# A transformer layer with an expert lookup on one Trainium2 core: SBUF sums for three output blocks only, a fourth gate tile loaded a block ahead, and a fourth tile for loads of u and v

## The chip, the cores and the metric

The kernel runs on one core of a Trainium2 chip. The metric is the device time of one execution in microseconds (us); before the change it is 3120.34 us, the median of three runs (3112.70 to 3122.46 us). A core has five engines with an instruction stream each: PE multiplies matrices, DVE (VectorE) and ACT (ScalarE) work on whole tiles, POOL (GpSimd) here issues gathers of table rows, and SP (SyncE) here issues nearly all other DMA transfers. Each stream is executed in its order, so an instruction that waits holds up everything behind it on that engine. SBUF holds 128 partitions of on-chip memory, PSUM the sums of PE.

## The reference, cut to what matters

One layer is computed for 1024 tokens of width 1024: attention, a convolution branch and, at the end, a product-key expert lookup, which takes most of the time. For each token 8 heads select 16 of 16384 experts each, with weights g, and

```
ue = take(u_tab, idx); ve = take(v_tab, idx)          # 128 rows of 1024 for each token
act = gelu(einsum('thkd,td->thk', ue, t))
out = einsum('thk,thkd->td', g * act, ve)
```

## The kernel before, in words

The tokens are two halves of 512. For the expert part the kernel does not gather rows for most tokens. It goes through all 16384 experts in 128 chunks of 128 and computes for all tokens of a half at once: `ups` = u chunk times h2 (24 matmuls, since each factor is split into two fp16 parts), `gel` = gelu of it, times a dense gate matrix that is zero where an expert was not selected, split into `wdh` (ACT) and `wdl` (DVE). The result times the v chunk is added to eight output blocks d of 128 rows. SUB = 4 chunks make a group, and a group's outputs are computed while the next group's chunks are prepared (`dense`).

Half 0 (`hf` = 0) does this for 512 tokens. Half 1 does it for 384 tokens and without `ups`: for these the products of u rows were gathered by POOL and multiplied on DVE beside half 0 (`dots`, tile `row`), and they are already in the gates. The last 128 tokens are done by gathers of u and v rows alone (`rows_out`, tile `racc`).

The gates lie in DRAM (`gd`, written by `build_g` from tile `ge`). They are read in blocks of GR = 8 chunks by two loads, one for each half q of the tokens, into tiles `gt`, of which there are three. `chunk` issues both loads when it comes to the first chunk of a block (lines 1081 to 1090). Loads of u and v (512 KB each) share the tag `uv32` with three tiles (lines 1096, 1105). Of the eight output blocks of half 0, five are kept in PSUM over all groups (`res`, NRES = 5); for the other three PE fills a `vps` bank in each group, which DVE adds to the SBUF tile `acc0`. `acc0` has room for all eight blocks (16 KB in each partition, line 1376). After half 0, `final` turns `acc0` into the output, while half 1 runs.

The order of the work around the change is made by a scheduler (Tile) that takes the instructions as the program lists them, with their tiles and pools, and sets the order in each engine's stream by its own estimate. A new tile of a tag, or a new pool at the address of a closed one, waits until what was there before is used up. `run_side` weaves the side streams (gates, gathered rows) between the steps of `dense`. Before the expert part come the key scores of half 1 (`scores`: tiles `sl`, `qql`, results `sv`, `si`), whose pools are closed just before the dense pools open; three chunks of u are split ahead (`u_first`, tiles `whl`).

Of the kernel before, what the change touches and what calls it, by code (L numbers as in the profile page):

```python
# [8 lines left out]
F32 = mybir.dt.float32  # L9
F16 = mybir.dt.float16  # L10
# [3 lines left out]
AF = mybir.ActivationFunctionType  # L14
# [4 lines left out]
D = 1024  # L19
L = 1024  # L20
CTX = 256
HALF = 512
# [5 lines left out]
TB = 8  # L28
REP = 4
NDENSE = 512  # L30
NMIX = 384
LATE_DOTS = 34
GATES_B = 0.64
GATES_D = 0.072
AHEAD = 1
GR = 8
DVE_ROWS = ((), tuple(range(8)), (), (1, 2, 3, 4, 5, 7))
W_FIRST = 6
UPRE = 3
SUB = 4  # L40
NGR = 128 // SUB
NRES = 5
# [67 lines left out]
class K:  # L110
# [841 lines left out]
    def build_g(self, t, hf):  # L952

        nc, p = self.nc, self.pg
        yield
        yield
        ii, g16 = self.slots(t, hf)
        yield
        late = []
        for q in range(128 // 16):  # L960
            ge = p.tile([128, 128, 16], F32, name="ge", tag="ge", bufs=self.ge_bufs)
            for sub in range(16 // TB):
                t0 = q * 16 + sub * TB
                ts = slice(t0, t0 + TB)

                def onehot(name, src, idx, op):
                    x = p.tile([128, TB, 128 // REP, REP], F16, name=name, tag=name, bufs=2)
                    nc.vector.tensor_tensor(x, src, idx[:, ts].unsqueeze(2).to_broadcast([128, TB, 128 // REP, REP]),
                                            op=op)
                    return x  # L970

                e1 = onehot("e1", self.iota, ii[:, 0], ALU.is_equal)
                ah = onehot("ah", e1, g16[:, 0], ALU.mult)
                al = onehot("al", e1, g16[:, 1], ALU.mult)
                e2 = onehot("e2", self.iota, ii[:, 1], ALU.is_equal)
# [27 lines left out]
    def open_gate(self, name, side, ge_bufs):  # L1003
        nc, a = self.nc, self.a
        self.ge_bufs = ge_bufs
        g, self.pg = self.pool(name, side=side)
        p = self.pg
        io32 = p.tile([128, 128], F32, name="io32")
        nc.sync.dma_start(io32, a["iota"])
        io16 = p.tile([128, 128], F16, name="iotas")  # L1010
        nc.vector.tensor_copy(io16, io32)
        self.iota = io16.rearrange("p (a b) -> p a b", b=REP).unsqueeze(1).to_broadcast([128, TB, 128 // REP, REP])
        self.cand = p.tile([128, 8, NCAND], F32, name="cand", tag="cand", bufs=1)
        nc.vector.memset(self.cand[:, :, 16:128], NEG)
        self.iota16 = p.tile([128, 16, 16], F16, name="iota16")
        nc.vector.tensor_copy(self.iota16, io32[:, 0:16].unsqueeze(2).to_broadcast([128, 16, 16]))
        return g
# [54 lines left out]
                pass  # L1072


    def chunk(self, hf, i1, p, pv):
# [5 lines left out]
        if self.gblock != (hf, i1 // GR):  # L1081
            self.gblock = hf, i1 // GR
            self.gts = []
            for q in range(2):
                gt = p.tile([128, nb, GR, 16], F32, name="gt", tag="gt", bufs=3)
                nc.sync.dma_start(
                    gt.rearrange("p b i t -> p b (i t)"),
                    self.gd[hf][nb * q:nb * q + nb].rearrange("b p i t -> p b (i t)")
                    [:, :, i1 // GR * GR * 16:(i1 // GR + 1) * GR * 16])
                self.gts.append(gt)  # L1090
        early = hf == 0 and i1 < UPRE
        if hf == 0 and not early:
            if i1 in self.u_first:
                uh, ul = self.u_first[i1]
            else:
                u32 = p.tile([128, 8, 128], F32, name="u32", tag="uv32", bufs=3)
                nc.sync.dma_start(u32, a["u_t"][i1])
                uh = p.tile([128, 8, 128], F16, name="uh", tag="uh", bufs=2)
                ul = p.tile([128, 8, 128], F16, name="ul", tag="ul", bufs=2)
                self.split(u32, 256.0, uh, ul)  # L1100
        late = []
        if hf and i1 in self.vparts:
            vh, vl = self.vparts[i1]
        else:
            v32 = p.tile([128, D], F32, name="v32", tag="uv32", bufs=3)
            nc.sync.dma_start(v32, a["v"][i1 * 128:(i1 + 1) * 128, :])
            vh = p.tile([128, D], F16, name="vh", tag="vh", bufs=2 * SUB)
            vl = p.tile([128, D], F16, name="vl", tag="vl", bufs=2 * SUB)
            nc.scalar.activation(vh, v32, AF.Copy, scale=16.0)  # L1109
            late.append((vl, v32, 16.0, vh))  # L1110
            if i1 >= 128 - 2 * SUB:
                self.vparts[i1] = vh, vl
        wh = self.pac.tile([128, nt], F16, name="wdh", tag="wdh", bufs=2 * SUB)
        wl = p.tile([128, nt], F16, name="wdl", tag="wdl", bufs=2 * SUB)
        if hf == 0:
            ge = p.tile([128, nt], F32, name="gel", tag="gel", bufs=2)
            if early:
                nc.sync.dma_start(ge, self.ged[i1])
            else:
                ps = pv.tile([128, 512], F32, name="ups", tag="v", bufs=3)  # L1120
                for k in range(8):
                    self.mm3(ps, uh[:, k, :], ul[:, k, :], hh[:, k, :], hl[:, k, :], k == 0, k == 7)
                nc.scalar.activation(ge, ps, AF.Gelu, scale=2.0 ** -12)
            gev = ge.rearrange("p (b t) -> p b t", t=16)
            for q in range(2):
                qs = slice(nb * q, nb * q + nb)
                nc.vector.tensor_mul(gev[:, qs, :], gev[:, qs, :], self.gts[q][:, :, i1 % GR, :])
            nc.scalar.activation(wh, ge, AF.Copy, scale=256.0)  # L1128
            late.append((wl, ge, 256.0, wh))
        else:  # L1130
            for q in range(2):
                qs = slice(nb * q, nb * q + nb)
                g = self.gts[q][:, :, i1 % GR, :]
                wq = wh.rearrange("p (b t) -> p b t", t=16)[:, qs, :]
                nc.scalar.activation(wq, g, AF.Copy, scale=256.0)
                late.append((wl.rearrange("p (b t) -> p b t", t=16)[:, qs, :], g, 256.0, wq))
        self.anchor = nc.vector.last
        for x in late:
            self.lo(*x)
        return vh, vl, wh, wl  # L1140

    def outputs(self, hf, gi, d, chunks, acc, pv):

        nc = self.nc
        nt = (NDENSE, NMIX)[hf]
        dsl = slice(d * 128, (d + 1) * 128)
        first, last = gi == 0, gi == NGR - 1
        if hf:
# [8 lines left out]
        po = po[:, :nt]  # L1157
# [3 lines left out]
        ad = acc[:, d, :nt]  # L1161
        if keep:
            if last:
                nc.scalar.activation(ad, po, AF.Copy)
        elif first:
            nc.vector.tensor_copy(ad, po)
        else:
            nc.vector.tensor_add(ad, ad, po)

    def outputs_mix(self, first, last, d, chunks, pv):  # L1170

# [16 lines left out]

    def dense(self, p, pv, accs):

        self.res, self.mix, self.vparts, self.gblock = {}, {}, {}, None
        prev = None
        for hf in range(2):
            for gi in range(NGR):
# [101 lines left out]
    def experts(self, p, pv, acc0):  # L1296

        rows = self.rows_stream()
        accs = [acc0, None]
# [3 lines left out]
        accs[1] = self.pc.tile([128, 8, HALF], F32, name="acc1", tag="h2")  # L1303
        self.run_side(self.ends(main, acc0, p), rows=rows, rate=(128 + LATE_DOTS) / 374.0)
        for _ in rows:
            pass
        self.last_group(accs[1], p, pv)

    def ends(self, main, acc0, p):
        last = self.final(acc0, p)  # L1310
# [7 lines left out]
    def run(self):  # L1318
# [60 lines left out]
        self.experts(pd, pv, acc0)  # L1379
        self.close(gd)  # L1380
        self.close(g_ac)
        self.close(g_g)
# [65 lines left out]
```

## Time and profile before

| what | value |
|---|---|
| three runs | 3112.70, 3120.34, 3122.46 us |
| profiled execution, own time | 3120.57 us |
| its span, first to last instruction | 3118.8 us |
| busy PE, DVE, ACT, POOL | 2913.7, 2631.9, 1180.7, 1067.5 us |
| mean granted PE clock | 0.977 |
| DMA moved | 795.75 MB, mean 255 GB/s |

Times in the profile count from the first instruction. The expert part starts with the first `ups` matmul at 1110.6 us; half 0 ends with the last `ups` at 2517.7 us. Busy time of PE is modelled: matmuls overlap at their ends. The granted clock is a share of the full 2.4 GHz; the lower level is 1.2 GHz, so a mean between 0.5 and 1 is a mix of both. "DMA" in a table of stretches is the mean busy share of the 16 DMA engines.

### The profile page before, as it was taken

To read this page: it belongs to the slowest core of one execution; us is meant where nothing else is said; L and a number is where in the kernel's file an instruction comes from. 1 tells how busy PE (TensorE), PEld (TensorE's weight loads), DVE (VectorE), ACT (ScalarE), POOL (GpSimd) and SP (SyncE) were. 2 spreads that over 40 slices of the span, in tenths; PEclk is the share of its full clock that TensorE was granted. 3 is DMA by queue.
4 is the path that set the end of the run, shared out by engine and by line. 5 is a ranking of instruction groups with operands and counts; after the bars stand their busy time and mean duration, and the time that the engine had idled before them with its cause. 6 is when DMAs were issued, how large, how long until landed. Compare 5 with 4: busy or idle time off the path is not lost. (4 is left out here: it accounts for less than half of the span.)

```text
span 3118.8 us, 49200 instructions
## 1 busy us (share of the span) xinstructions
PE 2913.7 (93%) x18685; PEld 1534.6 (49%) x18685; DVE 2631.9 (84%) x5438; ACT 1180.7 (38%) x1878; POOL 1067.5 (34%) x812
## 2 busy tenths in 40 slices
PE   6899999998899989999999999999999999999998
PEld 2455555444454444443444444344444456666665
DVE  7788666698899999899799988889988988777687
ACT  4744566333444332322333332333332333433332
POOL 2100011202231004444444544444444443444453
PEclk9999999999999999999999999999999999999999
DMA  6333334653445628898899998889898989999996
GB/s 218 95 110 111 112 116 152 234 183 136 174 191 196 234 87 307 280 317 303 303 316 335 345 325 297 295 318 342 315 335 304 336 287 341 328 323 326 333 321 225
DMA packets 327198, 795.75 MB, mean 255 GB/s; under 512 B 22961, under 2 KB 147249, under 8 KB 319793
## 3 DMA queue, kind: packets, MB, share of 16 engines
q1 hardware_dynamic: 222992, 397.25, 38.1%
q0 software_dynamic: 103968, 395.36, 34.8%
q8 instruction: 146, 2.39, 0.3%
q14 instruction: 92, 0.75, 0.1%
HBM read 696.31 MB, written 96.21 MB: 254 GB/s over the span
## 5 line engine op out<-in xcount | busy, mean ns | idle before, releaser
L904 POOL DMA_INDIRECT row<-u,ci x512 | 680.5, 1329 | 920.9 <-DVE row L67 685.0
L67 DVE SCALAR_TENSOR_TENSOR row<-row,hn 128x1024 f32<-128x1024 f32 x512 | 620.6, 1226 | 80.9 <-DMA row<-u,ci 75.0
L67 PE MATMUL res<-wdl,vh 128*128 128x128 f16 (+2 forms) x2176 | 629.3, 306 | 28.1 <-DVE wdl L67 28.0
L67 PEld LDWEIGHTS <-vh 128*128 128x128 f16 x5120 | 469.2, 98 | 340.0 <-issue 11.3
L67 PE MATMUL res<-wdh,vh 128*128 128x128 f16 (+2 forms) x2176 | 625.1, 306 | 3.3 <-ACT vh L1109 1.7
L67 PE MATMUL res<-wdh,vl 128*128 128x128 f16 (+2 forms) x2176 | 625.7, 306 | 0.8 <-DVE vl L67 0.8
L67 PE MATMUL ups<-h,uh 128*128 128x512 f16 x1952 | 589.8, 384 | 21.9 <-DVE acc L67 12.8
L67 PEld LDWEIGHTS <-whl 128*128 128x128 f16 x3288 | 315.1, 99 | 367.9 <-issue 41.9
L1109 ACT ACTIVATE vh<-v 128x1024 f16<-128x1024 f32 x248 | 258.4, 1052 | 484.9 <-DMA v<-v 433.6
L67 PE MATMUL ups<-h,ul 128*128 128x512 f16 x976 | 374.9, 384 | 21.1 <-DVE ul L67 21.1
L67 PE MATMUL bank<-hT,whl 128*128 128x512 f16 x1584 | 375.5, 386 | 15.7 <-ACT hT L331 5.7
L67 PEld LDWEIGHTS <-vl 128*128 128x128 f16 x2560 | 251.5, 98 | 205.0 <-issue 37.2
L67 DVE SCALAR_TENSOR_TENSOR vl<-v,vh 128x1024 f16<-128x1024 f32 x248 | 300.1, 1222 | 55.6 <-ACT vh L1109 53.1
L67 PEld LDWEIGHTS <-uh 128*128 128x128 f16 x1952 | 192.8, 99 | 258.0 <-issue 36.6
L904 POOL DMA_INDIRECT row<-v,ci x128 | 200.5, 1566 | 220.8 <-DVE racc L67 197.7
L140 ACT ACTIVATE uh<-u 128x1024 f16<-128x1024 f32 x122 | 128.4, 1052 | 311.1 <-PE ups L67 255.3
L1128 ACT ACTIVATE wdh<-gel 128x512 f16<-128x512 f32 x128 | 80.3, 629 | 371.4 <-DVE gel L67 353.3
L67 DVE SCALAR_TENSOR_TENSOR racc<-row,fig,racc 128x1024 f32<-128x1024 f32 x127 | 163.0, 1283 | 10.7 <-DMA row<-v,ci 9.7
L67 PEld LDWEIGHTS <-ul 128*128 128x128 f16 x976 | 96.6, 99 | 141.6 <-DVE ul L67 23.5
L67 DVE SCALAR_TENSOR_TENSOR ul<-u,uh 128x1024 f16<-128x1024 f32 x122 | 148.6, 1221 | 15.2 <-ACT uh L140 15.1
L67 PEld LDWEIGHTS <-e 128*128 128x128 f16 x1792 | 114.4, 99 | 94.4 <-issue 37.5
L67 DVE TENSOR_TENSOR e<-iotas,ii 128x1024 f16<-128x1024 f16 x224 | 145.4, 691 | 18.2 <-PE fbank L67 13.1
(230 smaller groups left out, 4192.6 us busy)
## 6 DMA issues: line engine op xcount, KB each, us to landing
v<-v SPq DMA_DIRECT2D x248, 512.0 KB, 6.5
u<-u_t SPq DMA_DIRECT2D x122, 512.0 KB, 6.7
gd<-ge POOLq DMA_DIRECT2D x32, 1024.0 KB, 4.4
gt<-gd SPq DMA_DIRECT2D x32, 1024.0 KB, 13.6
wm<-w_mod SPq DMA_DIRECT2D x48, 512.0 KB, 4.3
gd<-ge SPq DMA_DIRECT2D x24, 1024.0 KB, 8.6
gt<-gd SPq DMA_DIRECT2D x32, 768.0 KB, 11.0
w<-w_in SPq DMA_DIRECT2D x34, 512.0 KB, 4.2
```

The costliest lines, as they stand in the source:

```text
L67: r = f(*args, **kw)
L140: nc.scalar.activation(h, src, AF.Copy, scale=float(scale))
L904: self.nc.gpsimd.indirect_dma_start(out=r, out_offset=None, in_=tab, in_offset=bass.IndirectOffsetOnAxis(ap=ci[:, s:s + 1], axis=0))
L1109: nc.scalar.activation(vh, v32, AF.Copy, scale=16.0)
L1128: nc.scalar.activation(wh, ge, AF.Copy, scale=256.0)
```

## The change

Gate loads are issued by `load_gates`, for the next block, when chunk 2 (q = 0) and chunk 5 (q = 1) of the present block are listed, and there are four `gt` tiles. The tag `uv32` has four tiles. The room comes from `acc0`: during half 0 only three blocks have SBUF sums, in the tile `part`; the whole `acc0` is made at the end of half 0 at the address of h2, which is no longer read then, and `acc1` at the same address after it. `e1` of the gate builder has one tile in place of two, and the iota load shares the tile of `dot`.

```diff
+GATE_AT = (2, 5)
-                    x = p.tile([128, TB, 128 // REP, REP], F16, name=name, tag=name, bufs=2)
+                    x = p.tile([128, TB, 128 // REP, REP], F16, name=name, tag=name, bufs=1 if name == "e1" else 2)
-        io32 = p.tile([128, 128], F32, name="io32")
+        io32 = p.tile([128, 128], F32, name="io32", tag="dot", bufs=1)
+    def load_gates(self, hf, blk, q, p):
+        nb = (NDENSE, NMIX)[hf] // 32
+        if (hf, blk, q) not in self.gtiles:
+            gt = p.tile([128, nb, GR, 16], F32, name="gt", tag="gt", bufs=4)
+            self.nc.sync.dma_start(
...
+            self.gtiles[hf, blk, q] = gt
     def chunk(self, hf, i1, p, pv):
...
-            for q in range(2):
-                gt = p.tile([128, nb, GR, 16], F32, name="gt", tag="gt", bufs=3)
-                nc.sync.dma_start(
...
+            for q in range(2):
+                self.load_gates(hf, blk, q, p)
+            self.gts = [self.gtiles.pop((hf, blk, q)) for q in range(2)]
+        nxt = blk - 1 if hf else blk + 1
+        if 0 <= nxt < 128 // GR:
+            for q in range(2):
+                if (i1 + hf * SUB) % GR == GATE_AT[q]:
+                    self.load_gates(hf, nxt, q, p)
-                u32 = p.tile([128, 8, 128], F32, name="u32", tag="uv32", bufs=3)
+                u32 = p.tile([128, 8, 128], F32, name="u32", tag="uv32", bufs=4)
-            v32 = p.tile([128, D], F32, name="v32", tag="uv32", bufs=3)
+            v32 = p.tile([128, D], F32, name="v32", tag="uv32", bufs=4)
...
-        elif first:
+            return
+        ad = self.part[:, d - NRES, :]
+        if first:
             nc.vector.tensor_copy(ad, po)
         else:
-            nc.vector.tensor_add(ad, ad, po)
+            nc.vector.tensor_add(acc[:, d, :] if last else ad, ad, po)
...
+    def whole_acc(self, name):
+        return self.pc.tile([128, 8, HALF], F32, name=name, tag="h2")
...
-        acc0 = self.pac.tile([128, 8, HALF], F32, name="acc0")
+        self.part = self.pac.tile([128, 8 - NRES, HALF], F32, name="part")
```

In SP's stream of before, in half 1 at the start of a block: `gt_29143` is the second half of the block whose first chunk has the v tile `v32_29145`; `gt_29562` is the first half of the block after it.

```order
L1106 DMA v32_29078<-v 128x1024
L1106 DMA v32_29145<-v 128x1024
L1106 DMA v32_29187<-v 128x1024
L1106 DMA v32_29226<-v 128x1024
L1086 DMA gt_29143<-gd384_93 128x12x128
L1086 DMA gt_29562<-gd384_93 128x12x128
```

The same place in the changed kernel: `gt_29226` and `gt_29396` are both halves of the block after, whose first chunk has `v32_29566`.

```order
L1119 DMA v32_29145<-v 128x1024
L1119 DMA v32_29187<-v 128x1024
L1119 DMA v32_29228<-v 128x1024
L1119 DMA v32_29291<-v 128x1024
L1081 DMA gt_29226<-gd384_93 128x12x128
L1081 DMA gt_29396<-gd384_93 128x12x128
L1119 DMA v32_29354<-v 128x1024
L1119 DMA v32_29398<-v 128x1024
L1119 DMA v32_29437<-v 128x1024
L1119 DMA v32_29500<-v 128x1024
L1119 DMA v32_29566<-v 128x1024
```

A half of a block that stood three rows behind the v load of its own first chunk now stands five rows ahead of it; both halves stand together at the border of the block before, not at its chunks 2 and 5.

SP's stream of before, where the expert part begins: the loads of the first chunks (`gt_11995`, `v32_11999`, `gel_12006`) stand between the last weights of the score stage (`whl`).

```order
L1086 DMA gt_11995<-gd512_92 128x16x128
L1086 DMA gt_11997<-gd512_92 128x16x128
L800 DMA h2d_89<-hn_11306 128x4x128
L157 DMA whl_11418<-ws_sk1_6811 128x2048
L1106 DMA v32_11999<-v 128x1024
L1118 DMA gel_12006<-ged0_10238 128x512
L157 DMA whl_11455<-ws_wq9_6853 128x2048
L1106 DMA v32_12024<-v 128x1024
```

The same place in the changed kernel, from the last weight on:

```order
L158 DMA whl_11851<-ws_wq15_7279 128x2048
L161 DMA w32_11963<-u_t 128x1024
L1010 DMA io32_11987<-iota 128x128
L914 DMA hn2_12442<-h2d_89 128x1024
L1081 DMA gt_11995<-gd512_92 128x16x128
L1081 DMA gt_11997<-gd512_92 128x16x128
L1119 DMA v32_11999<-v 128x1024
L1131 DMA gel_12006<-ged0_10238 128x512
L1119 DMA v32_12024<-v 128x1024
L1131 DMA gel_12031<-ged1_10272 128x512
L1081 DMA gt_12048<-gd512_92 128x16x128
L1119 DMA v32_12050<-v 128x1024
```

All loads of the expert part moved behind all loads of the score stage. The first of them, `gt_11995`, now lies where `whl` and `w32` tiles were, and it waits for the last `ups` matmul that reads the third split chunk of u (`whl_11962`).

DVE's stream of before in the score stage has work of the first chunks between two rounds of the key search (`sl`):

```order
L67 MAX_INDEX si1_86<-sv1_85,sl_11433 128x8 x4
L67 TENSOR_TENSOR gel_12006<-gel_12006,gt_11995 128x256
L67 TENSOR_TENSOR gel_12006<-gel_12006,gt_11997 128x256
L67 SCALAR_TENSOR_TENSOR vl_12002<-v32_11999,vh_12001 128x1024
L67 SCALAR_TENSOR_TENSOR qql_11483<-bank_11457,qqh_11482 128x512
L67 MAX sv1_85<-sl_11499 128x8 x4
```

In the changed kernel it stands behind the last round (`sl_11930`):

```order
L68 MAX_INDEX si1_86<-sv1_85,sl_11930 128x8 x4
L68 MEMSET cand_11991 128x8x112
L68 TENSOR_SCALAR g2r_30863<-g2s_83 128x8
L68 CAST iotas_11989<-io32_11987 128x128
L68 CAST iota16_11993<-io32_11987 128x256
L68 TENSOR_TENSOR gel_12006<-gel_12006,gt_11995 128x256
L68 TENSOR_TENSOR gel_12006<-gel_12006,gt_11997 128x256
L68 SCALAR_TENSOR_TENSOR vl_12002<-v32_11999,vh_12001 128x1024
```

Seven `vl`, one `ul` and four `gel` instructions left the score stage in this way.

## Rows read from the trace of the kernel before

**Rows 1.** The page's first line: span of the profiled execution.
```profile
span 3118.8 us, 49200 instructions
```
**Rows 2.** Busy time by stretch: length, engines' busy (instructions), PE clock, DMA share, GB/s.
```profile
1130.00:1200.00 70.00, 62.29 (x279) 27.46 (x278) 59.84 (x187) 21.31 (x28) 18.45 (x15) 0.95 0.55 184
1200.00:2518.00 1318.00, 1266.81 (x6283) 590.86 (x6282) 1172.70 (x2053) 420.19 (x566) 608.42 (x459) 0.98 0.89 316
...
2560.00:3096.00 536.00, 506.95 (x4538) 351.20 (x4536) 416.81 (x585) 192.59 (x371) 248.29 (x163) 0.98 0.91 321
```
**Rows 3.** Waits of PE, 2560 to 3096: sum in us, times, longest.
```profile
PE res L67 <- DVE wdl L67: 26.5, 16, 3.4
```
**Rows 4.** Waits of ACT in the same stretch.
```profile
ACT wdh L1135 <- DMA gt<-gd: 109.7, 14, 10.9
```
**Rows 5.** Waits of DVE in the same stretch.
```profile
DVE wdl L67 <- ACT wdh L1135: 67.6, 13, 9.3
```
**Rows 6.** Timeline of SP's DMA issues at one block's start: start, length, what.
```profile
2740.34 3.46 SPq L1086 DMA_DIRECT2D gt<-gd  x2
```
**Rows 7.** Timeline of ACT, same place; in brackets the idle time before.
```profile
2750.73 0.36 ACT L1135 ACTIVATE wdh<-gt 128x192 f16<-128x192 f32 x1 [9.90 <-DMA gt<-gd]
```
**Rows 8.** Timeline of PE, same place.
```profile
2761.34 0.48 PE L67 MATMUL res<-wdl,vh 128*128 128x384 f16 x1 [3.42 <-DVE wdl L67]
```
**Rows 9.** Busy time by stretch, right behind that wait.
```profile
2760.00:2768.00 8.00, 6.66 (x24) 3.30 (x24) 6.91 (x8) 3.63 (x8) 5.80 (x5) 0.57 0.93 336
```
**Rows 10.** Waits of DVE in half 0, 1200 to 2518.
```profile
DVE row L67 <- DMA row<-u,ci: 58.8, 60, 3.8
DVE vl L67 <- ACT vh L1109: 24.7, 10, 6.1
DVE wdl L67 <- ACT wdh L1128: 24.3, 9, 4.7
DVE ul L67 <- ACT uh L140: 15.1, 13, 2.2
DVE gel L67 <- DMA gt<-gd: 9.1, 4, 3.0
```
**Rows 11.** Timeline of ACT in half 0, where a load of v is late.
```profile
1271.79 1.06 ACT L1109 ACTIVATE vh<-v 128x1024 f16<-128x1024 f32 x1 [11.65 <-DMA v<-v]
1272.75 0.61 ACT L1128 ACTIVATE wdh<-gel 128x512 f16<-128x512 f32 x1
```
**Rows 12.** Busy time by stretch from the score stage to the first outputs.
```profile
1060.00:1100.00 40.00, 35.93 (x218) 18.16 (x217) 40.00 (x207) 13.88 (x20) 0.00 (x0) 1.00 0.51 176
1100.00:1110.00 10.00, 3.88 (x32) 2.54 (x31) 10.00 (x43) 3.86 (x7) 0.00 (x0) 0.74 0.19 53
...
1120.00:1130.00 10.00, 9.23 (x44) 4.10 (x43) 7.42 (x31) 1.15 (x2) 0.00 (x0) 1.00 0.50 166
```
**Rows 13.** DVE's groups, 1060 to 1112: count, busy us, mean ns.
```profile
L67 DVE SCALAR_TENSOR_TENSOR vl<-v,vh 128x1024 f16<-128x1024 f32 x7 | 8.6, 1239 | 0.0
```
**Rows 14.** Instructions on gel, 1060 to 1110: ns min/median/max, first and last start.
```profile
L67 DVE TENSOR_TENSOR gel<-gel,gt x4: 427/436/443, 1064.7 to 1072.1; 128x256 f32<-128x256 f32 x4
```
**Rows 15.** The ups matmuls of the chunks split ahead, same columns.
```profile
L67 PE MATMUL ups<-h,whl x72: 379/379/631, 1110.6 to 1128.1; 128*128 128x512 f16 x72
```
**Rows 16.** SP's issue of the first two gate tiles, timeline.
```profile
1036.90 4.14 SPq L1086 DMA_DIRECT2D gt<-gd  x2
```
**Rows 17.** DMA issues, 1036 to 1042: count, KB each, median us to landing.
```profile
gt<-gd SPq DMA_DIRECT2D x2, 1024.0 KB, 8.9
```
**Rows 18.** Timeline of PE at the first outputs.
```profile
1129.27 1.02 PE L67 MATMUL res<-wdh,vh 128*128 128x512 f16 x4 [0.77 <-ACT wdh L1128]
```
**Rows 19.** Busy time by stretch where the DMA engines moved most in 50 us.
```profile
2600.00:2650.00 50.00, 46.17 (x402) 31.28 (x400) 39.77 (x62) 16.73 (x29) 17.79 (x13) 0.97 1.02 354
...
2150.00:2200.00 50.00, 49.11 (x264) 23.69 (x263) 46.14 (x75) 15.73 (x22) 24.62 (x18) 1.00 0.97 359
```

More of the change, by code (lines that the diff above doesn't have):

```diff
@@ L1072, in run_side @@
                 pass
+    def load_gates(self, hf, blk, q, p):
[3 more added lines that the diff above has]
+            self.nc.sync.dma_start(
+                gt.rearrange("p b i t -> p b (i t)"),
+                self.gd[hf][nb * q:nb * q + nb].rearrange("b p i t -> p b (i t)")
+                [:, :, blk * GR * 16:(blk + 1) * GR * 16])
+            self.gtiles[hf, blk, q] = gt
     def chunk(self, hf, i1, p, pv):
@@ L1080, in chunk @@
         hh, hl = self.h2h[0], self.h2l[0]
-        if self.gblock != (hf, i1 // GR):
-            self.gblock = hf, i1 // GR
-            self.gts = []
+        blk = i1 // GR
+        if self.gblock != (hf, blk):
+            self.gblock = hf, blk
             for q in range(2):
-                gt = p.tile([128, nb, GR, 16], F32, name="gt", tag="gt", bufs=3)
-                nc.sync.dma_start(
[L1087 to L1090, printed above, removed]
+                self.load_gates(hf, blk, q, p)
[5 more added lines that the diff above has]
+                    self.load_gates(hf, nxt, q, p)
         early = hf == 0 and i1 < UPRE
@@ L1144, in outputs @@
         nc = self.nc
-        nt = (NDENSE, NMIX)[hf]
         dsl = slice(d * 128, (d + 1) * 128)
@@ L1156, in outputs @@
             po = pv.tile([128, 512], F32, name="vps", tag="v", bufs=3)
-        po = po[:, :nt]
         for i, (vh, vl, wh, wl) in enumerate(chunks):
@@ L1160, in outputs @@
                      i == SUB - 1 and (last or not keep))
-        ad = acc[:, d, :nt]
         if keep:
             if last:
-                nc.scalar.activation(ad, po, AF.Copy)
-        elif first:
+                nc.scalar.activation(acc[:, d, :], po, AF.Copy)
+            return
+        ad = self.part[:, d - NRES, :]
+        if first:
             nc.vector.tensor_copy(ad, po)
         else:
-            nc.vector.tensor_add(ad, ad, po)
+            nc.vector.tensor_add(acc[:, d, :] if last else ad, ad, po)
     def outputs_mix(self, first, last, d, chunks, pv):
@@ L1189, in dense @@
     def dense(self, p, pv, accs):
-        self.res, self.mix, self.vparts, self.gblock = {}, {}, {}, None
+        self.res, self.mix, self.vparts, self.gblock, self.gtiles = {}, {}, {}, None, {}
         prev = None
@@ L1294, in last_group, with experts @@
                 nc.sync.dma_start(ov[:, k - 1:k + 1, HALF:HALF + NMIX], acc[:, k - 1:k + 1, :NMIX])
-    def experts(self, p, pv, acc0):
+    def whole_acc(self, name):
+        return self.pc.tile([128, 8, HALF], F32, name=name, tag="h2")
+    def experts(self, p, pv):
         rows = self.rows_stream()
-        accs = [acc0, None]
+        accs = [None, None]
         main = self.dense(p, pv, accs)
@@ L1302, in experts @@
         self.run_side(islice(main, steps), self.gates_stream(), GATES_D, rows, (512 - LATE_DOTS) / (steps - 15.0), (1, 0))
-        accs[1] = self.pc.tile([128, 8, HALF], F32, name="acc1", tag="h2")
-        self.run_side(self.ends(main, acc0, p), rows=rows, rate=(128 + LATE_DOTS) / 374.0)
+        accs[0] = self.whole_acc("acc0")
+        self.run_side(self.ends(main, accs[0], p), rows=rows, rate=(128 + LATE_DOTS) / 374.0)
         for _ in rows:
             pass
-        self.last_group(accs[1], p, pv)
+        self.last_group(self.whole_acc("acc1"), p, pv)
     def ends(self, main, acc0, p):
@@ L1375, in run @@
         g_ac, self.pac = self.pool("acc", side="left")
-        acc0 = self.pac.tile([128, 8, HALF], F32, name="acc0")
+        self.part = self.pac.tile([128, 8 - NRES, HALF], F32, name="part")
         gd, pd = self.pool("dense0", side="left")
         g_g = self.open_gate("gate1", "right", 1)
-        self.experts(pd, pv, acc0)
+        self.experts(pd, pv)
         self.close(gd)
```

## The prediction, made before the changed kernel ran

> **What bounds the kernel now.** I read the table of busy time by stretch first, then the waits of PE, then those of the engines that PE waits for, then timelines at single places. In both halves of the expert part PE is the engine that sets the end: it is busy 1266.81 of 1318 us in half 0 and 506.95 of 536 us in half 1, more than any other, and the granted clock is 0.98 [rows 2]. What can be won is what PE loses. In half 1 that is 536 − 506.95 = 29 us of standing, and 0.02 x 507 = 10 us of running at the lower clock, 39 us in all. In half 0 it is 51 us of standing and 0.02 x 1267 = 25 us, 76 us in all.
>
> In half 1 the cause is one chain, and the reader can follow it at one block's start. SP issues the two gate loads at 2740.34 [rows 6]. ACT, which needs the tile for `wdh`, stands 9.90 us for it [rows 7]; ACT's vh work is queued behind that wait. DVE stands for `wdh` (`wdl`, 67.6 us in 13 waits [rows 5]), and PE, which has a little work ahead, stands 3.42 us at the end of the chain [rows 8]. Behind the wait the granted clock is 0.57 over 8 us, so much of these 8 us ran at 1.2 GHz [rows 9]. Over the half ACT waits 109.7 us for gates [rows 4], and 26.5 of PE's 29 us of standing wait for `wdl` [rows 3].
>
> In half 0 no single wait rules. DVE is busy 1172.70 of 1318 us [rows 2], and each time it stands it gets behind, which PE feels a little later at `ul`, at a `vps` bank or at the gate builder. Its waits are 58.8 us for gathered rows, and 24.7 + 24.3 + 15.1 + 9.1 = 73.2 us in 36 waits for things that hang on loads of v, u and gates [rows 10]. That `wdl` belongs to these shows at 1271.79: ACT stands 11.65 us for a load of v, and the `wdh` behind it in ACT's stream, which DVE needs, comes only then [rows 11].
>
> **The change, part by part.**
>
> *Gate tiles, half 1.* The order puts both halves of a block a whole block ahead of use, eight chunks. A block lasts 536 / 16 = 33 us at most here, and a pair of loads needs some 10 us from issue to use [rows 6, 7]. So the wait of ACT goes, with it that of DVE for `wdh` and the 26.5 us of PE, and most of the 10 us at the lower clock, which follow these waits. What is late next is a load of v: 1.5 MB of gates still go through SP's queue in one piece in front of four v loads. But there are four `uv32` tiles now, so a v load starts one chunk (4 us) earlier than it did. I take three quarters of the 39 us: −29. Bounds: −39, all of it, and −5, if the loads that were waited for are only replaced by others.
>
> *Loads of u and v, half 0.* A chunk is 48 of the 6283 matmuls in 1318 us [rows 2], so 10 us or a little more, and has two of these loads; the fourth tile starts each about 5 us earlier. DVE's 36 waits on loads average 73.2 / 36 = 2.0 us, the longest is 6.1 [rows 10]; 5 us cover most of them. The same for the gates (four waits, 9.1 us). Of DVE's waits listed, 58.8 + 73.2 = 132 us, the loads have 55%; 55% of PE's 76 us is 42. The 58.8 us for gathered rows stay, and the bursts of gate selection on DVE stay. I take half of the 42: −20. Bounds: −42, and +15 if earlier loads of u and v make the gathers later by as little as a quarter of what they cost now (58.8 / 4).
>
> *The start of the expert part.* Here the change costs time. In before the loads of gates, v and `gel` run beside the score stage; now `gt_11995` waits for the last `ups` on `whl_11962`, and all loads of the expert part are queued behind it on SP. Two effects go against each other.
>
> First, the score stage gets shorter. DVE is busy without a break in it (40.00 of 40, 10.00 of 10 us), and PE only 3.88 of 10 us at its end [rows 12]. Seven `vl` at 1.24 us, a `ul` of the same shape and four `gel` at 0.43 us leave it [rows 13, 14]: 8 x 1.24 + 4 x 0.43 = 11.6 us, about 10 as they overlap at their ends. PE has 35.93 + 3.88 = 39.8 us of work in these 50 us, so it cannot gain more than 10 either. The first `ups` then starts at about 1101 in place of 1110.6 [rows 15]. The 72 `ups` took 17.9 us with part of them at a clock of 0.74; at 0.216 us each they take 15.6 and end at about 1116.6.
>
> Second, PE then has nothing to do. From that moment the gate pair has to be loaded. In before a pair was issued in 4.14 us [rows 16] and landed 8.9 us (median) behind its issue [rows 17]; I take 10.5 us from the first issue to the second landing. Behind it come v (0.5 MB) and `gel` (0.25 MB), which at 354 GB/s [rows 19] are 2.1 us. Then two `gel` products and one `wdh`, 2 x 0.43 + 0.61 [rows 14, 11]: first output at 1116.6 + 10.5 + 2.1 + 1.5 = 1130.7. In before it stood at 1129.27 [rows 18]. The next chunks arrive one at a time, and the order puts a 1 MB gate load of the next block in front of the third v: 1 MB / 354 = 3 us, of which PE has work for a part. I add 4 us for this: PE is about 5 to 6 us later than before. DVE is idle from about 1110 to 1127 where before it stood only 2.6 us [rows 12], and has the 10 us of moved work still to do, but it got to the end of the scores 10 us earlier: net 17 − 2.6 − 10 = 4 us behind. I take half of that. Sum +8. Bounds: −6, if the loads land faster in an idle queue and a later wait of PE in 1130 to 1200 (7.7 us of standing there [rows 2]) is absorbed; +25, if PE's and DVE's delays add.
>
> *The rest.* The adds into `part` are as many as into `acc0`, on the same engine. `acc0` at h2's address waits for the last `ups`, which stands ahead of the last outputs in PE's stream anyway; `acc1` waits for the stores of `acc0`, some 400 us before it is written. One `e1` tile is written and read by DVE alone, in its order, so it adds no wait; it shifts a few instructions of the score stage by a place or two. 0, bounds −6 and +6.
>
> *Sum.* The profiled execution took 3120.57 us by its own time, 3118.8 of it span [rows 1], and the median is 3120.34, so no correction is needed. 3120.6 − 29 − 20 + 8 = 3079.6: **3080 us**.
>
> **The rivals.**
>
> *The DMA engines are the bound behind PE.* Half 1 moves 321 GB/s x 536 us = 172 MB at a share of 0.91 [rows 2]. The fullest stretches show 354 GB/s at a share of 1.02 and 359 at 0.97 [rows 19]. At 354 the half needs at least 486 us, at my forecast (507) it would run at 339, 96% of that. If queues that full delay v and rows as gates were delayed, half 1 gains 10 instead of 29 and half 0 nothing but 8 to cover the start: 3120.6 − 10 − 8 + 8 = 3111. For it: the share is near 1 already. Against it: PE's waits in half 1 name `wdl` behind gates, hardly vh or vl [rows 3].
>
> *The start costs more, half 0 gives nothing.* If DVE's select work, queued behind the late gates, delays the first gathers and PE meets that again, the start costs 20; if the waits of half 0 come from DVE's own bursts, 0 there: 3120.6 − 29 + 20 = 3112.
>
> *Slower: loads of u and v crowd out the gathers.* SP's queue with four tiles keeps more load in flight beside POOL's queue of gathered rows, which has four tiles as before. DVE takes 459 rows in half 0, as many as POOL issues there [rows 2], and waits at 60 of them. If each comes later by 0.15 us on average, DVE stands 69 us more, and PE loses 76 / 132 = 0.58 us for each us that DVE stands: +40. With the start (+8) and half 1 gaining 10: 3120.6 + 40 + 8 − 10 = 3159. It decides from about 0.05 us per row on that half 0 has no gain left. For it: rows are DVE's longest wait. Against it: the bytes are the same, and a queue that is half a chunk further ahead asks for no more per chunk than before.
>
> The Trainium skill (DMA: Bandwidth & Descriptors, "Queues, rings and completion order") has a rule that speaks for this rival: each DMA engine takes turns, packet by packet, between the queues that have work for it, so a gather gets half of an engine as long as SP's queue is not empty. By the rule the gathers would lose in the measure in which SP's queue is empty less often than before, in the direction of the 3159 us above. No row here tells the two queues apart on one engine; the row waits of half 0, at 58.8 us before, will.
>
> *The change does not do what it says.* The order shows gate loads a block ahead, but not spread over chunks 2 and 5; that costs a burst, counted above under v.
>
> **How the numbers follow.** Forecast 58%, by itself 3060 to 3100. DMA bound 14%, dear start 18%, slower 10%. The range 3052 to 3116 takes the bounds of half 1 and half 0 together at the low end and the two middle rivals at the high end; it leaves out most of the slow rival and a little on each side. About 0.3% (9 us) is what a measurement of this kernel tells from no change. Faster by more than that means below 3111: the forecast and half of the two middle rivals, 0.75. Within it 0.16, slower 0.09.
>
> **What would show it.** In the profile after, in half 1, ACT's wait of 109.7 us for gates is near 0, PE's wait for `wdl` below 8 us, and the stretch some 29 us shorter. In half 0, DVE's waits for vh, uh and wdh fall from 64 us to about 30 and its wait for rows stays near 59. At the start the first `ups` stands at about 1101, and PE then stands some 14 us in one piece before the first output, for `wdh` behind the gate loads. I am wrong if half 1 keeps its waits under another name (vh behind v), if row waits grow, or if the hole at the start is over 25 us.

## The result, and the profile after

The changed kernel takes 3086.6 us (median of four runs, 3085.71 to 3087.36), the kernel before 3120.05 us in the runs beside it (3112.70 to 3122.46): a ratio of 0.9895, with a 95% interval of 0.9875 to 0.9915. That is 1.05% or 33.5 us less; 3080 was predicted. The sum was nearly right. Its terms were not, and two of their errors cancelled; most of the experiments are on that.

The first line of the page, beside [rows 1]:

```profile
span 3085.6 us, 49211 instructions
```

Busy time by stretch in the changed kernel, with the columns of [rows 2]:

```profile
1100.00:1110.00 10.00, 10.00 (x48) 4.46 (x47) 5.80 (x36) 0.00 (x0) 0.00 (x0) 0.99 0.18 61
...
1200.00:1500.00 300.00, 266.38 (x1161) 116.20 (x1159) 251.87 (x518) 79.34 (x101) 134.20 (x99) 0.94 0.83 283
1500.00:2518.00 1018.00, 998.78 (x5083) 471.52 (x5084) 924.42 (x1555) 341.93 (x467) 476.92 (x362) 0.99 0.91 326
2560.00:3060.00 500.00, 498.39 (x4525) 349.44 (x4525) 420.89 (x592) 189.01 (x381) 252.41 (x166) 1.00 0.96 348
```

The two stretches of half 0 in the kernel before, which [rows 2] have as one:

```profile
1200.00:1500.00 300.00, 282.96 (x1283) 126.42 (x1282) 269.42 (x538) 87.30 (x110) 142.00 (x106) 0.98 0.86 300
1500.00:2518.00 1018.00, 983.85 (x5001) 464.44 (x5000) 903.28 (x1517) 332.90 (x457) 466.42 (x354) 0.99 0.90 321
```

In half 1 PE stands 1.6 us in 500 us, at a clock of 1.00; before, 29 in 536 at 0.98. In half 0 a gain and a loss cancel: from 1200 to 1500 PE stands 300 − 266.38 = 33.6 us where it stood 17.0, and from 1500 to 2518 19.2 us where it stood 34.2. From 1200 to 1500 the granted clock is also lower, 0.94 against 0.98.

In absolute times, the last `ups` of half 0 ends 8 us later than before (the two lines are before and after), and from there to the end of the span it takes 3085.6 − 2525.7 = 559.9 us, where it took 601.1:

```profile
L67 PE MATMUL ups<-h,ul x976: 377/379/634, 1141.1 to 2517.7; 128*128 128x512 f16 x196
```
```profile
L68 PE MATMUL ups<-h,ul x976: 377/379/634, 1155.1 to 2525.7; 128*128 128x512 f16 x196
```

So half 1 gave 41 us, and all that comes ahead of it lost 8. The waits of PE, and behind them those of ACT, in half 1 (2560 to 3060) of the changed kernel, beside [rows 3] and [rows 4]; the last line is one of the kernel before (2560 to 3096) that [rows 4] leave out:

```profile
PE res L68 <- ACT wdh L1148: 1.1, 1, 1.1
PE res L68 <- DVE wdl L68: 0.8, 1, 0.8
```
```profile
ACT vh L1122 <- PE res L68: 230.3, 25, 10.8
...
ACT vh L1122 <- DMA v<-v: 22.8, 14, 9.8
...
ACT wdh L1148 <- DMA gt<-gd: 0.7, 1, 0.7
```
```profile
ACT vh L1109 <- DMA v<-v: 156.2, 63, 10.1
```

Before, ACT waited not only 109.7 us for gates but also 156.2 us for loads of v, more than for gates. In the changed kernel 0.7 and 22.8 us of these are left, and ACT now waits for PE to free its tiles: it is ahead.

The start. PE in the changed kernel, beside [rows 15] and [rows 18]; then SP's issues, whose second column is how long the issue took:

```profile
1096.10 17.70 PE L68 MATMUL ups<-h,whl 128*128 128x512 f16 x72 [0.73 <-ACT sl L811]
1126.29 1.01 PE L68 MATMUL res<-wdh,vh 128*128 128x512 f16 x2 [12.48 <-ACT wdh L1141]
```
```profile
1113.83 1.62 SPq L1081 DMA_DIRECT2D gt<-gd  x2
1115.50 4.21 SPq L1119 DMA_DIRECT2D v<-v  x1
1119.74 0.43 SPq L1131 DMA_DIRECT2D gel<-ged  x1
```

DVE meanwhile, busy only 5.80 us between 1100 and 1110 where it had no break before [rows 12], stands 17.8 us for the first `gel` (waits, 1060 to 1130), and the first gather of half 1's rows starts 7 us later than before (POOL's timelines, before and after):

```profile
DVE gel L68 <- DMA gel<-ged: 17.8, 1, 17.8
```
```profile
1165.91 1.65 POOL L904 DMA_INDIRECT row<-u,ci  x1 [135.49 <-DVE acc L67]
```
```profile
1172.88 3.92 POOL L905 DMA_INDIRECT row<-u,ci  x1 [147.02 <-ACT wdh L1141]
```

The last view is worked out from ACT's timeline: the 125 `gel` activations, one for each chunk of half 0 that computes `ups`, mark its pace. The table gives how much later than in the kernel before each kernel is at the 1st, the 11th and so on, and the time from the last `ups` to the end of the span (us, of the profiled executions). The kernels below the changed one are those of the experiments.

| kernel | 1st | 11th | 26th | 61st | 125th | then to the end of the span |
|---|---|---|---|---|---|---|
| before (times) | 1131 | 1230 | 1400 | 1795 | 2518 | 601 |
| changed | +0 | +24 | +31 | +26 | +8 | 560 |
| gates_three_tiles | +2 | +25 | +34 | +30 | +10 | 597 |
| uv_three_tiles | −1 | +22 | +28 | +31 | +32 | 599 |
| part_alone | +4 | +27 | +36 | +43 | +48 | 594 |
| rows_in_order | +5 | +30 | +31 | +38 | +24 | 566 |
| vl_beside_part | −7 | +14 | +17 | +10 | −9 | 564 |
| uh_beside_part | 0 | 0 | −3 | −6 | −26 | 561 |
| uh_beside_part_three_tiles | −7 | −1 | +14 | +18 | +24 | 584 |
| single_e1_in_before | −9 | −10 | −9 | −7 | −1 | 595 |

The changed kernel loses 31 us in the first 26 chunks, 24 of them in the first 11, and wins 23 back in the other 99. These are single executions, some of them up to 10 us off their kernel's median (rows_in_order: 3109.86 against 3099.89), so differences of a few us between rows say nothing.

### The profile page after: what moved, and what is told of

Its sections match the earlier page's. It is cut to its first block, busy times and chain, and to the rows that moved or that the text cites. A ratio compares the mean times of both kernels' runs of the same rounds, so it can differ in the third digit from the quotient of the medians.

```text
span 3085.6 us, 49211 instructions
## 1 busy us (share of the span) xinstructions
PE 2911.7 (94%) x18685; PEld 1528.7 (50%) x18685; DVE 2636.4 (85%) x5438; ACT 1174.5 (38%) x1878; POOL 1054.1 (34%) x812
## 4 chain that ended last, share of the span: by engine, by line
PE 41%; DVE 22%; issue 18%; POOL 10%; DMA 7%; ACT 2%; SPq 0%; POOLq 0%; DVEq 0%; ACTq 0%
PE res L68 19%; PE bank L68 11%; POOL row L905 10%; PE ups L68 4%; PE sc L68 4%; DMA row<-u,ci 4%; DVE row L68 2%; DVE e L68 2%; DVE si L68 2%; DVE eq L68 2%; PE vps L68 1%; DVE sv L68 1%; DVE ah L68 1%; DVE al L68 1%; DVE sl L68 1%
## 5 line engine op out<-in xcount | busy, mean ns | idle before, releaser
L68 PEld LDWEIGHTS <-vh 128*128 128x128 f16 x5120 | 468.9, 98 | 362.3 <-issue 25.9
L68 PE MATMUL ups<-h,ul 128*128 128x512 f16 x976 | 374.5, 384 | 17.9 <-DVE ul L68 17.8
L68 DVE SCALAR_TENSOR_TENSOR ul<-u,uh 128x1024 f16<-128x1024 f32 x122 | 148.4, 1219 | 21.5 <-ACT uh L141 17.1
L995 ACT ACTIVATE ge<-fbank 128x512 f32<-128x512 f32 x224 | 121.1, 592 | 96.3 <-PE fbank L68 75.3
```

Source lines behind the costliest of these rows:

```text
L68: r = f(*args, **kw)
L995: nc.scalar.activation(ge[:, :, o:o + 4], ps.rearrange("p t i -> p i t"), AF.Copy, scale=2.0 ** -12)
```

## The experiments

Each was timed in turn with the kernel before on one chip. There were four groups on four chips: the first four experiments with each other, the next four, the two of `uh_beside_part`, and the last alone. Medians of different groups compare only loosely, to a few us. The first theory, from the changed kernel's waits, was that DVE takes gathered rows out of turn. From 1200 to 1500 DVE's wait for rows had grown, before and after:

```profile
DVE row L67 <- DMA row<-u,ci: 16.0, 18, 3.4
```
```profile
DVE row L68 <- DMA row<-u,ci: 36.3, 16, 6.0
```

POOL gathers `row_12664`, `row_12714`, `row_12717`, `row_12732`, `row_12749` in this order; in the changed kernel DVE's stream has

```
L68 SCALAR_TENSOR_TENSOR row_12664,dot_12444<-row_12664,hn2_12442 128x1024
L68 SCALAR_TENSOR_TENSOR row_12749,dot_12444<-row_12749,hn2_12442 128x1024
L68 SCALAR_TENSOR_TENSOR row_12714,dot_12444<-row_12714,hn2_12442 128x1024
```

There are four `row` tiles, so the gather of `row_12749` is issued only once `row_12664` is used up, and DVE then waits out a whole gather. The kernel before has no such place among its first 33 rows.

**rows_in_order.**

```diff
+from contextlib import nullcontext
...
-            nc.vector.scalar_tensor_tensor(r, r, 0.0625, hn, op0=ALU.mult, op1=ALU.mult,
-                                           accum_out=dot[:, s:s + 1])
+            with self.tc.issue_after(self.dot_before) if s else nullcontext():
+                nc.vector.scalar_tensor_tensor(r, r, 0.0625, hn, op0=ALU.mult, op1=ALU.mult,
+                                               accum_out=dot[:, s:s + 1])
+            self.dot_before = nc.vector.last
```

> The changed kernel (3086.6 us), with one thing more: each product of a gathered u row on DVE is queued behind the one before it, so DVE takes the rows in the order in which POOL gathers them. In the changed kernel DVE's stream has 17 places where a row stands up to three places ahead of its turn, 8 of them among the first 50 rows; in the kernel before there were 11, none of them before the 33rd row. Theory A (out-of-turn rows drain the four row tiles and cost the early part of half 0 its time): DVE's waits for rows in 1060 to 1500 fall from 45.7 to about 22 us, PE's loss in 1200 to 1500 falls from 33.6 to about 17 us, and the time to about 3068 us (3060 to 3076). Theory B (loads of u and v, further ahead, crowd the gathers): the row waits stay at 40 us or more and the time at 3083 to 3090. Theory C (DVE is behind from the late start): row waits may fall, but PE's loss up to 1500 stays above 28 us and the time at 3081 to 3090.

Measured: 3099.89 us (3094.77 to 3109.86), ratio 0.9926 (0.9903 to 0.9949). DVE's waits from 1200 to 1500:

```profile
DVE vl L69 <- ACT vh L1125: 25.9, 7, 6.5
DVE row L69 <- DMA row<-u,ci: 14.6, 18, 1.7
```

The row waits went from 36.3 to 14.6 us as theory A had it, and the time did not fall (it is 10 us above that of changed_again below, with intervals that just overlap): DVE waits for `vh` in their place, 25.9 us where it was 9.5. Theory A explains the waits and not the loss: at the 26th chunk the lag is 31 us here too. As the edit also holds up `vl` behind rows, this alone does not show that the order of rows costs nothing. Theory B falls: the loads of u and v run as far ahead here as in the changed kernel, and the gathers are not late. And with three tiles for u and v (uv_three_tiles below) the row waits of the same stretch stay long:

```profile
DVE row L68 <- DMA row<-u,ci: 29.7, 20, 6.8
```

**gates_on_need.** The load-ahead lines are off, with four gate tiles.

```diff
+AHEAD_GATES = False
...
-        if 0 <= nxt < 128 // GR:
+        if AHEAD_GATES and 0 <= nxt < 128 // GR:
```

> The changed kernel without the lines that list the gate loads of the next block at chunks 2 and 5: both loads are listed at the first chunk of their block, as before the change, but there are four gate tiles. In SP's order the two loads of a block then still stand five v loads ahead of its first chunk, because their tiles are free there. Theory A (the fourth tile alone brings the gain of half 1): time 3084 to 3090, no gap of PE for wdl in half 1, half 1 about 560 us from the last ups to the end. Rival (the lines that list the loads ahead bring it): half 1 goes back towards 601 us and the time to 3115 to 3130.

Measured: 3089.2 us (3077.76 to 3091.58), ratio 0.9887 (0.9844 to 0.9931); PE waits 1.5 us for `wdl` in half 1, and from the last `ups` to the end it takes 560 us. Of the change to the gate loads the fourth tile is the whole effect, as theory A had it: SP's order puts a load where its tile becomes free.

**gates_three_tiles.** As gates_on_need, with `bufs=3` for `gt`.

> As gates_on_need, and with three gate tiles; the room of the fourth is left empty. Four tiles for u and v stay. Theory A (the gate tile is all of half 1's gain): half 1 takes about 600 us from the last ups to the end, ACT waits some 110 us for gates there again, and the time is about 3086.6 + 41 = 3127 us (3118 to 3132), slower than the kernel before, since half 0 is 11 us slower in the changed kernel. Rival (the fourth tile for v has part of it, as v loads no longer stand behind gates): half 1 takes 575 to 590 us and the time is 3100 to 3115.

Measured: 3120.17 us (3111.83 to 3130.9), ratio 1.0008 (0.9985 to 1.0031), as theory A had it. ACT in half 1 (2560 to 3060):

```profile
ACT vh L1123 <- PE res L69: 127.4, 19, 12.3
ACT wdh L1149 <- DMA gt<-gd: 106.9, 14, 12.3
ACT vh L1123 <- DMA v<-v: 31.9, 22, 3.4
```

**uv_three_tiles.** The changed kernel with `bufs=3` for `u32` and `v32`.

> The changed kernel with three tiles for loads of u and v; four gate tiles a block ahead stay. Theory A (the fourth tile for u and v gives the later part of half 0 what it gained): PE's loss in 1500 to 2518 goes from 19 us back to about 30, and half 1 loses a little as v loads are later: time 3096 to 3105. Theory B (loads that run further ahead crowd the gathers): DVE's waits for rows fall in half 0 and the time falls to 3065 to 3080. Theory D (with gates out of the way three tiles are enough, the gain was the gates'): 3083 to 3091.

Measured: 3149.51 us (3135.35 to 3160.18), ratio 1.0089 (1.0062 to 1.0115): slower than the kernel before, and by far more than any theory said. ACT in half 1 (2560 to 3060):

```profile
ACT vh L1122 <- DMA v<-v: 226.6, 64, 12.2
ACT vh L1122 <- PE res L68: 32.2, 14, 7.9
```

Read the two together. With three gate tiles ACT still waits for gates; with four gate tiles but three for v it waits for v, 226.6 us where it was 156.2 in the kernel before. Either tile alone leaves half 1 at 597 or 599 us of the 601; both give 560. In half 0 the fourth `uv32` tile is worth 32 − 8 = 24 us, all of it behind the 26th chunk, and the gate tile nothing. Both hold beside a fourth tile of the other kind: against part_alone below, which has neither and ends half 0 at +48, the `uv32` tile is worth 38 us and the gate tile 16. Of the 32 us that uv_three_tiles loses by the end of half 0, 28 are there by the 26th chunk: something in the change that is none of these tiles costs nearly 30 us at the start.

The second theory: the hole at the start. PE's part of it is short (12.5 us, and the scores end earlier). DVE's is not: it has 17.8 us of standing, and the seven `vl`, the `ul` and the four `gel` that the kernel before does in the score stage are still to do.

**vl_beside_part.** One tile moved: gates and v then no longer lie where the last weights are read, and the first loads run beside the score stage again.

```diff
-            vl = p.tile([128, D], F16, name="vl", tag="vl", bufs=2 * SUB)
+            vl = self.pac.tile([128, D], F16, name="vl", tag="vl", bufs=2 * SUB)
```

> The changed kernel with the eight vl tiles in the pool of part, behind it: the gate and v tiles now lie above the weights of the score stage, and the first loads of gates, v and gel stand among that stage's weights again, as before the change. The products on gel are then done while PE still works on the scores; wdh and vl still wait for the last ups. Theory C (the late first loads leave DVE idle for 17.8 us and set the stream of gathered rows back, which half 0 does not make up): the hole of PE before the first output shrinks from 12.65 to 3 to 5 us, the first gather comes at about 1158 in place of 1172.9, the last ups at about 2508 in place of 2525.7, and the time is about 3070 us (3060 to 3078). Rival D (the early part of half 0 is bound by the pace of rows and v loads alone, whenever it starts): the last ups stays within 5 us of 2526 and the time at 3082 to 3092.

Measured: 3071.93 us (3070.22 to 3074.36), ratio 0.9843 (0.9826 to 0.9859). PE at the start, and DVE's waits from 1060 to 1200:

```profile
1101.52 18.04 PE L68 MATMUL ups<-h,whl 128*128 128x512 f16 x72 [0.73 <-ACT sl L811]
1120.28 1.02 PE L68 MATMUL res<-wdh,vh 128*128 128x512 f16 x4 [0.72 <-ACT wdh L1141]
```
```profile
DVE row L68 <- DMA row<-u,ci: 9.7, 4, 7.4
DVE vl L68 <- PE ups L68: 4.9, 1, 4.9
```

The wait of 17.8 us for the first `gel` is gone, and the longest wait of DVE there that is not for rows is 4.9 us. 17.7 us come off the time (beside changed_again). Rival D falls. There is still a lag of 17 us at the 26th chunk, though the first gather stands at 1163.2, 2.7 us ahead of the kernel before: late gathers are not what carries this lag.

**vl_beside_part_rows_in_order.** Both edits.

> vl_beside_part, and rows on DVE in the order of their gathers as in rows_in_order. Theory C: in the changed kernel the order of rows changed nothing for the better, since DVE then waited for v instead (vl 9.5 to 25.9 us); with the start mended v is not late and the order of rows is worth its 20 us of waits or part of them: 3050 to 3066 us. Rival (rows in turn hold up vl and ul behind them wherever they are late, and cost 13 us as they did in rows_in_order): 3080 to 3090 us.

Measured: 3076.59 us (3066.13 to 3084.1), ratio 0.9848 (0.9826 to 0.9871): not to be told from vl_beside_part, and between the ranges of theory C and of its rival. Putting the rows in their turn is worth nothing here either, and with this the order of rows falls as the cause.

**part_alone.** Three tiles of each kind, and the gates listed on need; the smaller sums, the single `e1`, the iota load in the tile of `dot` and the late loads stay.

> The changed kernel without its two gains: three gate tiles, listed on need, and three tiles for u and v; the smaller sums, the single e1 tile and the late first loads stay. Theory C: the last ups is at about 2550 us as with uv_three_tiles, 32 us later than in the kernel before, and half 1 takes 601 us as before: 3150 us (3142 to 3158). Rival (the start costs 8 us as predicted, and what uv_three_tiles lost in half 0 comes from gate loads that stand ahead of v loads): 3122 to 3134 us.

Measured: 3153.81 us (3145.95 to 3163.2), ratio 1.0101 (1.007 to 1.0131). As theory C had it: 34 us slower than the kernel before.

**changed_again.** The changed kernel on the chip of vl_beside_part and part_alone.

> The changed kernel as it is, on the chip of the experiments, to compare with: 3086.6 us as before, 3082 to 3092.

Measured: 3089.63 us (3084.02 to 3091.41), ratio 0.9903 (0.9887 to 0.992).

**uh_beside_part.** `part`, `uh` and `ul`, which are needed last, over the weights that are read last; `wdh` and `wdl` behind them.

```diff
+    def u_tiles(self):
+        return [self.pac.tile([128, 8, 128], F16, name=n, tag=n, bufs=2) for n in ("uh", "ul")]
...
-                uh = p.tile([128, 8, 128], F16, name="uh", tag="uh", bufs=2)
-                ul = p.tile([128, 8, 128], F16, name="ul", tag="ul", bufs=2)
+                uh, ul = self.u_tiles() if self.u_next is None else self.u_next
+                self.u_next = None
...
-        wl = p.tile([128, nt], F16, name="wdl", tag="wdl", bufs=2 * SUB)
+        wl = self.pac.tile([128, nt], F16, name="wdl", tag="wdl", bufs=2 * SUB)
...
         self.part = self.pac.tile([128, 8 - NRES, HALF], F32, name="part")
+        self.u_next = self.u_tiles()
```

> The changed kernel with another order of tiles in SBUF: the tiles that are needed last (part, uh, ul) lie over the split weights of u that are read last, wdh and wdl behind them, and gates, v and vl above. Now wdh and vl no longer wait for the last ups either, DVE's stream has its first five vl in the score stage as before the change, and its rows stand out of turn in 11 places as before, not 17. Theory C (all that half 0 lost early comes from loads and DVE work that the layout pushed behind the score stage): the lag behind the kernel before, 17 us at chunk 25 in vl_beside_part and 31 in the changed kernel, is near 0 here, the last ups comes at about 2494 us (before 2517.7, less the 24 us that the fourth tile for u and v gives), half 1 takes 560 us, and the time is about 3056 us (3048 to 3064). Rival E (DVE cannot do the moved work any earlier, since it is busy without a break in the score stage): as vl_beside_part, 3067 to 3075 us.

Measured: 3054.64 us (3044.69 to 3056.7), ratio 0.9767 (0.9745 to 0.9789). Busy time by stretch:

```profile
1200.00:1500.00 300.00, 283.40 (x1286) 126.73 (x1287) 272.98 (x545) 90.52 (x115) 144.65 (x109) 0.98 0.86 301
1500.00:2480.00 980.00, 963.84 (x4920) 455.64 (x4919) 888.66 (x1492) 326.55 (x448) 450.63 (x346) 0.99 0.91 327
2530.00:3030.00 500.00, 498.64 (x4534) 349.90 (x4533) 419.70 (x593) 187.93 (x374) 254.66 (x165) 1.00 0.95 345
```

PE stands 16.6 us from 1200 to 1500, as in the kernel before (17.0), and the lag at the 26th chunk is −3 us. Rival E falls, and with four tiles of each kind theory C holds: this version beats both kernels, by some 35 us the changed one, from nothing but which tile lies on which. The layout takes away two things at once, the late loads and work, and the rows out of turn (DVE's row waits from 1200 to 1500):

```profile
DVE row L68 <- DMA row<-u,ci: 18.9, 18, 2.9
```

That the second is worth nothing by itself is what vl_beside_part_rows_in_order shows.

**uh_beside_part_three_tiles.** The same with three tiles of each kind.

> uh_beside_part with three gate tiles, listed on need, and three tiles for u and v: the layout with part, and nothing of the gains. Theory C: the 34 us that part_alone lost were the layout at the start and nothing else of the change, so this is the kernel before, 3120 us (3113 to 3127). Rival F (part, the single e1 tile or the row order costs time by itself): 3132 to 3145 us.

Measured: 3129.3 us (3119.87 to 3156.62), ratio 1.0033 (1.0009 to 1.0058). This lies between the ranges of theory C and rival F. By the medians 24.5 of the 34 us of part_alone are the layout; some 7 to 10 us are left that theory C has no place for. The table shows that these hide more. This execution ends half 0 24 us later than the kernel before, though it starts 7 us early, and takes 584 us from there to the end, 17 less than the 601. So without the fourth tiles the layout does not bring half 0 back to the kernel before, and the tiles are worth some 50 us in half 0 and 23 in half 1 in this layout, where part_alone and the changed kernel have 40 and 34 between them.

**single_e1_in_before.** The kernel before with `bufs=1 if name == "e1" else 2`.

> The kernel before with one e1 tile in place of two in the gate builder, and nothing else of the change. uh_beside_part_three_tiles was slower than the kernel before by 0.33% (0.09 to 0.58%), 10 us, without any of the late loads. If the single e1 tile is that, the time is 3126 to 3134 us; if it costs nothing, as the prediction had it (DVE alone writes and reads it, in its order), 3116 to 3124 us, and the 10 us belong to part or to the order of the tiles.

Measured: 3111.64 us (3098.61 to 3120.85), ratio 0.9969 (0.9953 to 0.9985). It is not the single `e1`, which alone is even 0.3% faster. What the 7 to 10 us are, and the 24 us of half 0 behind them, stays open: `part`, the iota load in the tile of `dot`, or where the other tiles lie.

## Why the prediction was right, and where it was not

- **The sum.** 3118.8 − 41 − 24 + 32 = 3085.8 us of span, against 3085.6: half 1, the fourth `uv32` tile in half 0, and all else that comes ahead of the last `ups`. Predicted were −29, −20 and +8. Two terms came out better and one much worse; that the time came within 7 us of the forecast was luck, by their cancelling. Only the −41 and the 8 us lost ahead of it are read from the two kernels. How the 8 divide is taken from uv_three_tiles, and by other pairs of runs the parts are larger or smaller, as the tiles and the layout change each other's worth.
- **Half 1, −29 predicted, −41 measured.** The signs came as forecast: ACT's gate wait fell from 109.7 to 0.7 us, PE's wait for `wdl` from 26.5 to 0.8, the clock rose from 0.98 to 1.00. The mis-sized step is "I take three quarters": the bound of 39 us was reached, and about 2 more came from 2518 to 2560. But the cause was not one chain. ACT waited 156.2 us for v in the same stretch, which the prediction does not count; it has v late only "next", and holds back a quarter for it. The fourth `uv32` tile, which was to help there, did more than help: uv_three_tiles shows that without it nothing is left of the gain, and gates_three_tiles that with it alone there is none either. The forecast held because the change brought both tiles.
- **Half 0's loads, −20 predicted, −24 measured** (last `ups` at 2549.7 in uv_three_tiles, at 2525.7 in the changed kernel). The size was near, the working was not: the waits did not behave as said. DVE's waits for vh, uh and wdh were to fall from 64 to about 30 us; they are 31.8 + 17.1 + 4.0 = 52.9. DVE's waits in the changed kernel, 1200 to 2518, beside [rows 10]:

```profile
DVE row L68 <- DMA row<-u,ci: 75.6, 56, 6.0
DVE vl L68 <- ACT vh L1122: 31.8, 10, 5.8
DVE ul L68 <- ACT uh L141: 17.1, 16, 2.5
...
DVE wdl L68 <- ACT wdh L1141: 4.0, 2, 3.3
```

  What went is `wdl`, 24.3 to 4.0, and `gel` for gates, 9.1 to nothing; the waits for `vl` and `ul` grew. In uv_three_tiles the `wdl` wait of the same stretch is back, all of it behind 1500:

```profile
DVE wdl L68 <- ACT wdh L1141: 26.3, 6, 9.3
```

  So the fourth `uv32` tile took away this one wait of the 73.2 us that the prediction counted on, and the −20 came near by luck.
- **The start, +8 predicted, +32 in this sum.** This step failed. The hole of PE was sized well: 14 us and a first output at 1130.7 predicted, 12.5 us and 1126.3 measured (the first `ups` stood 5 us earlier than the 1101 predicted, and the 72 took 17.7 us and not 15.6). The failure is the line on DVE: "net 17 − 2.6 − 10 = 4 us behind". It credits DVE with reaching the end of the scores 10 us earlier, but it got there by leaving 10 us of work undone, and that work comes after. The credit and the debt cancel: 17 − 2.6 = 14.4 us behind, by the prediction's own numbers. Then half of the 4 was taken, as if half 0 had room to make it up. It has little early on: DVE is busy 269 of 300 us there in the kernel before. The lag grew to 24 us by the 11th chunk and 31 by the 26th, and half 0 did not pay it back by itself (uv_three_tiles keeps +32 to the end). vl_beside_part and uh_beside_part take it away in two steps, some 18 and 17 us. By which path it grows from 14 to 31 us is not shown. The first gather, 7 us late, is not the path: vl_beside_part has it 2.7 us early with a lag of 17 us, uh_beside_part 2.2 us late (1168.1) with none.
- **The rest, 0 predicted.** It is not 0. With the start mended and three tiles of each kind 7 to 10 us of time are left over the kernel before (0.33%, 0.09 to 0.58%), and 24 us at the end of half 0 in the one execution that was traced. How much of the 32 is this and not the start stays open.
- **The rival "the DMA engines are the bound"** is out: half 1 runs at 348 GB/s, close to the 354 that it was held against, and PE loses 1.6 us in 500.
- **The rival "the start costs more, half 0 gives nothing"** named the right engine, DVE with its work queued behind late gates, and priced it at 20 us where it was up to 32; the first gathers, by which it was to reach PE, are not the path. It was wrong on half 0, whose 24 us are real and show once the start is mended (uh_beside_part ends half 0 26 us ahead of the kernel before).
- **The slower rival, gathers crowded out,** is out, although row waits in half 0 did grow, 58.8 to 75.6 us. All of the growth is between 1200 and 1500 (16.0 to 36.3); behind that, where u and v run as far ahead, the wait is 39.3 us against 42.7. And rows_in_order takes the growth away with the loads unchanged, while uv_three_tiles, with fewer loads in flight, keeps most of it (29.7 us). The Trainium skill's rule of queues that take turns on an engine (DMA: Bandwidth & Descriptors, "Queues, rings and completion order") would have made the gathers later wherever SP's queue is fuller; these waits do not show it.
- **The rival "it does not do what it says"** was half right, and harmless: the lines that list gate loads ahead do nothing beyond the fourth tile (gates_on_need).

## What to carry to other kernels

When a change moves work of a busy engine past a point, the time gained ahead of the point is the work itself, not a gain: count the standing in between, and count it in full while that engine has little room. Two buffers in front of one engine can each be worth next to nothing alone and 40 us together, so list all that the engine waits for, and take one buffer away at a time before saying which brought the gain. When tiles change size, look at what now lies on the tiles that are read last before a stage border: the first loads of the next stage wait there, and the tiles that are needed last should lie there instead. Here that was worth some 35 us.

## What was not expected of the hardware

SP's issue of a v load, 0.33 us in the middle of half 0, took 4.21 us right behind the two gate loads at 1115.50, and the small `gel` load that DVE stood for could be issued only after it.
